# Add and GELU of two 1024 x 4096 matrices: which rows of HBM go to which partition

## The chip, the cores and the metric

The kernel runs on one core of a Trainium2 chip. The metric is the device time of one execution in microseconds. Three runs of the kernel before gave a median of 120.16 us (120.15 to 120.21).

## The reference

```python
batch, dim = 1024, 4096          # x, y: float32
z = x + y
return (0.5 * z * (1 + np.tanh(np.sqrt(2 / np.pi) * (z + 0.044715 * z ** 3)))).astype(np.float32)
```

Everything is elementwise: no value depends on its neighbours. Each of x, y and the output has 16.78 MB; 33.55 MB are read and 16.78 MB written.

## The kernel before, in words

Each matrix is seen as 128 rows of 128 KB, one row per partition: partition p holds the bytes from p x 128 KB on (`"(p n) d -> p (n d)"`). A row has TOT = 32768 floats, and HALF = 16384 floats is 64 KB. The tile z in SBUF has room for all of x and is overwritten by the sum and then by the result; the tile y holds half of y and is used twice.

There are six transfers, all issued from SyncE (SP), each 128 partitions of 64 KB, 8 MB in all. Their order is the list `sp`: first half of y (`load_y`, line 135), both halves of x (`load_x`, line 130), second half of y (line 135), first half of the output and second half (`store`, line 139). The second load of y waits until all adds that read the first half of y are done, because it writes the same tile. A store waits for the last GELU of its half. `begin_early` puts the issue of the first two loads ahead of the kernel's body; `wait_late` moves the wait for the last store behind the other end work.

The compute is cut into 20 chunks of 512 to 2048 columns. An add (line 150) is done by VectorE, or by GpSimd for chunks 7, 8 and 12. For eight chunks ScalarE copies x into PSUM first (`copy`, line 143), and the add reads that operand from PSUM. ScalarE then applies the GELU in place (line 162). The order on each engine is written out by hand in the lists `sp`, `pool`, `dve` and `acts`, and is issued under a manual schedule.

Of the kernel before, what the change touches and what calls it, by code (L numbers as in the profile page):

```python
# [66 lines left out]
def kernel(  # L67
# [12 lines left out]
    nc = tc.nc  # L80
    P = nc.NUM_PARTITIONS
# [3 lines left out]
    N, D = x.shape  # L85
    assert N % P == 0
    TOT = N // P * D
    xv, yv, ov = (a.rearrange("(p n) d -> p (n d)", p=P) for a in (x, y, out))

    HALF = TOT // 2  # L90
    xloads = [HALF, HALF]
    yloads = [16384, 16384]
    stores = [16384, 16384]
# [17 lines left out]
    def over(rs, lo, hi):  # L111
        return [i for i, (a, b) in enumerate(rs) if a < hi and b > lo]
# [6 lines left out]
    zt = pool_sb.tile([P, TOT], fp32, tag="z", name="z")  # L119
    yt = pool_y.tile([P, HALF], fp32, tag="y", name="y")  # L120
    ps = pool_ps.tile([P, 4096], fp32, tag="ps", name="ps")
# [5 lines left out]

    def load_x(i):
        a, b = xr[i]
        nc.sync.dma_start(out=zt[:, a:b], in_=xv[:, a:b])  # L130

    def load_y(i):
        a, b = yr[i]
        o = a % HALF
        nc.sync.dma_start(out=yt[:, o : o + b - a], in_=yv[:, a:b])  # L135

    def store(i):
        a, b = sr[i]
        nc.sync.dma_start(out=ov[:, a:b], in_=zt[:, a:b])

    def copy(c):
        a, b = cr[c]
# [2 lines left out]
    def add(c):  # L145
        a, b = cr[c]
        o = a % HALF
        eng = nc.gpsimd if c in on_gpsimd else nc.vector
# [15 lines left out]
    def earlier_user(c):  # L164
        lo, hi = copies[c], copies[c] + chunks[c]
        before = [k for k in copies if k < c and copies[k] < hi and copies[k] + chunks[k] > lo]
        return [(add, k) for k in before]

    sp = [(load_y, i) for i in over(yr, 0, HALF)] + [(load_x, 0), (load_x, 1)]
    sp += [(load_y, i) for i in over(yr, HALF, TOT)]  # L170
    sp += [(store, i) for i in range(len(stores))]
    pool = [(add, c) for c in on_gpsimd]
    dve = [(add, c) for c in on_vector]
# [3 lines left out]
        load_x: lambda i: [],  # L177
        load_y: lambda i: [(add, c) for c in over(cr, yr[i][0] - HALF, yr[i][1] - HALF)],
        copy: lambda c: [(load_x, i) for i in over(xr, *cr[c])] + earlier_user(c),
        add: lambda c: [(load_x, i) for i in over(xr, *cr[c])]  # L180
        + [(load_y, i) for i in over(yr, *cr[c])]
        + [(copy, k) for k in copies if k == c]
        + [(add, k) for h, k in held.items() if h == c],
# [55 lines left out]
```

## Time and profile before

| | us |
|---|---|
| median of three runs (lowest, highest) | 120.16 (120.15, 120.21) |
| span of the profiled execution, first to last instruction | 118.7 |
| median less span | 1.5 |
| VectorE busy | 29.1 |
| ScalarE busy | 44.1 |
| GpSimd busy | 13.8 |
| the DMA queue's packets, share of 16 DMA engines' span | 98.5% |
| issue to landing, median: y, x, output | 23.6, 50.1, 21.6 |
| HBM traffic over the span | 424 GB/s |

The profile is of one execution, and gives its span; of what lies around the span (1.5 us) it shows nothing, and the profiled execution has no time of its own beside the span. Busy time of an engine is time in which it executed; issues of DMAs are rows of SP's queue (SPq) and not busy time. "Landing" is when the semaphore of a transfer is complete. A window is a stretch of the span, with the busy time of each engine in it, the share of time in which the 16 DMA engines had a packet, and the GB/s.

### The profile page before, as it was taken

How to read it: one execution, taken by the hardware profiler on the slowest of the kernel's cores; microseconds unless marked ns; L12 is line 12 of the kernel's file. 1: busy time of each engine (PE TensorE's matmuls, PEld its weight loads, DVE VectorE, ACT ScalarE, POOL GpSimd, SP SyncE). 2: the span in 40 equal slices, each digit the busy share in tenths (PEclk: the TensorE clock that was granted, in tenths of full speed). 3: DMA queues.
4: the chain of work that ended last, by engine and by line, in shares of the span. 5: the costliest groups of instructions: out<-in, count | busy, mean ns of one | idle time of the engine just before them, and what ended most of it. 6: DMA issues, size and time to landing. Idle time of an engine off the chain costs nothing.

```text
span 118.7 us, 112 instructions
## 1 busy us (share of the span) xinstructions
DVE 29.1 (25%) x18; ACT 44.1 (37%) x30; POOL 13.8 (12%) x7
## 2 busy tenths in 40 slices
DVE  0000000000000099994000000009999920000000
ACT  5000000000000096792059999903799980000000
POOL 0000000000000029980000000009500000000000
DMA  9889988998899888998899888998899888988891
GB/s 353 353 375 641 398 353 353 596 464 353 353 420 618 376 353 353 618 442 353 353 508 552 353 353 375 641 398 353 353 552 508 353 353 353 707 353 353 353 641 66
DMA packets 864, 50.33 MB, mean 424 GB/s; under 512 B 96, under 2 KB 96, under 8 KB 96
## 3 DMA queue, kind: packets, MB, share of 16 engines
q1 hardware_dynamic: 864, 50.33, 98.5%
HBM read 33.55 MB, written 16.78 MB: 424 GB/s over the span
## 4 chain that ended last, share of the span: by engine, by line
DMA 56%; DVE 14%; ACT 10%; DVEq 1%; ACTq 0%; SPq 0%; issue 0%
DMA z<-in_x_dram 34%; DMA y<-in_y_dram 21%; DVE z L150 14%; ACT z L162 10%; DVEq L206 1%; ACTq L206 0%; SPq L135 0%; DVEq L150 0%
## 5 line engine op out<-in xcount | busy, mean ns | idle before, releaser
L162 ACT ACTIVATE z<-z 128x2048 f32<-128x2048 f32 (+3 forms) x20 | 29.7, 1555 | 5.5 <-DVE z L150 5.5
L143 ACT COPY ps<-z 128x2048 f32<-128x2048 f32 (+2 forms) x8 | 13.0, 1654 | 46.8 <-DMA z<-in_x_dram 45.1
L150 DVE TENSOR_TENSOR z<-z,y 128x2048 f32<-128x2048 f32 (+2 forms) x9 | 13.6, 1574 | 40.0 <-DMA z<-in_x_dram 40.0
L150 DVE TENSOR_TENSOR z<-ps,y 128x2048 f32<-128x2048 f32 (+2 forms) x8 | 15.6, 2016 | 25.4 <-DMA y<-in_y_dram 25.4
L150 POOL TENSOR_TENSOR z<-z,y 128x2048 f32<-128x2048 f32 x3 | 13.5, 4529 | 70.7 <-DVE z L150 43.4
L191 ACT ACT_TABLE_LOAD x1 | 1.3, 1283 | 1.3 <-PEq L223 1.3
L190 DVE MEMSET one<- 128x1 f32 x1 | 0.1, 59 | 1.3 <-PEq L223 1.3
L191 ACT ACTIVATE one<-one 128x1 f32<-128x1 f32 x1 | 0.2, 203 | 0.0
L223 POOL MEMSET const-float32-0.0<- 128x1 f32 x1 | 0.1, 99 | 0.2 <-issue 0.2
L223 POOL MEMSET const-bfloat16-1.0<- 128x1 bf16 x1 | 0.1, 102 | 0.0
L223 POOL MEMSET const-uint8-127<- 128x1 uint8 x1 | 0.1, 102 | 0.0
L223 POOL MEMSET const-float32-1.0<- 128x1 f32 x1 | 0.1, 99 | 0.0
## 6 DMA issues: line engine op xcount, KB each, us to landing
y<-in_y_dram SPq DMA_DIRECT2D x2, 23.6
z<-in_x_dram SPq DMA_DIRECT2D x2, 50.1
out_dram<-z SPq DMA_DIRECT2D x2, 21.6
```

The costliest lines, as they stand in the source:

```text
L143: nc.scalar.copy(out=in_psum(c), in_=zt[:, a:b])
L150: ins = eng.tensor_add(out=zt[:, a:b], in0=first, in1=yt[:, o : o + b - a])
L162: nc.scalar.activation(out=zt[:, a:b], in_=zt[:, a:b], func=act.Gelu_apprx_tanh)
L190: nc.vector.memset(one[:, :1], 0.0)
L191: nc.scalar.activation(out=one[:, :1], in_=one[:, :1], func=act.Gelu_apprx_tanh)
L206: tc.compile()
L223: nc = _bacc.Bacc("TRN2", target_bir_lowering=False, num_devices=1)
```

## The change

Half h of the columns of the tile now comes from another place in HBM. Partition p = 8q + j, with q from 0 to 15 and j from 0 to 7. Before, half h of partition p was the 64 KB at p x 128 KB + h x 64 KB. After, it is the 64 KB at q x 1 MB + h x 512 KB + j x 64 KB. So the eight partitions of a group still share 1 MB of each matrix, but half 0 of these eight partitions is the first 512 KB of it, without a gap, and half 1 the second 512 KB. x, y and the output are laid out alike. Nothing else is edited.

```diff
-    xv, yv, ov = (a.rearrange("(p n) d -> p (n d)", p=P) for a in (x, y, out))
-
     HALF = TOT // 2
+    Q = 16
+
+    def rows(array, lo, hi):
+        h = lo // HALF
+        assert hi <= (h + 1) * HALF
+        own = array.rearrange("n d -> (n d)").rearrange("(q h j c) -> h q j c", q=Q, h=2, j=P // Q)
+        return own[h][:, :, lo - h * HALF : hi - h * HALF]
+
...
     def load_x(i):
         a, b = xr[i]
-        nc.sync.dma_start(out=zt[:, a:b], in_=xv[:, a:b])
+        nc.sync.dma_start(out=zt[:, a:b], in_=rows(x, a, b))

     def load_y(i):
         a, b = yr[i]
         o = a % HALF
-        nc.sync.dma_start(out=yt[:, o : o + b - a], in_=yv[:, a:b])
+        nc.sync.dma_start(out=yt[:, o : o + b - a], in_=rows(y, a, b))

     def store(i):
         a, b = sr[i]
-        nc.sync.dma_start(out=ov[:, a:b], in_=zt[:, a:b])
+        nc.sync.dma_start(out=rows(out, a, b), in_=zt[:, a:b])
```

In the built program the pattern of a transfer was 128x16384 (rows by floats) on both sides. It is now 16x8x16384 on the HBM side, with 1 MB between the sixteen and 64 KB between the eight, and 128x1x16384 on the SBUF side.

## The prediction

> **What bounds the kernel now.** I read the page first: busy shares and slices, then the chain that ended last, then the windows cut at the landings, then the queue's own issues.
>
> ```profile
> span 118.7 us, 112 instructions
> DVE 29.1 (25%) x18; ACT 44.1 (37%) x30; POOL 13.8 (12%) x7
> DMA packets 864, 50.33 MB, mean 424 GB/s; under 512 B 96, under 2 KB 96, under 8 KB 96
> q1 hardware_dynamic: 864, 50.33, 98.5%
> ```
>
> No engine is busy for half the span, while the one queue's packets fill 98.5% of the time of 16 DMA engines. Take off the 96 tiny packets: 768 packets carry 50.33 MB, 65,536 bytes each. That is one packet for each 64 KB partition row of the six transfers (6 x 128), 48 on each DMA engine if they are dealt evenly. One takes about 0.985 x 16 x 118.7 / 768 = 2.44 us, which is 27 GB/s on one DMA engine.
>
> ```profile
> 4.20:21.90 17.70, 0.00 (x0) 0.00 (x0) 0.00 (x0) 1.00 1.08 467
> 21.90:41.30 19.40, 0.00 (x0) 0.00 (x0) 0.00 (x0) 1.00 1.00 432
> 41.30:60.70 19.40, 13.35 (x7) 11.21 (x7) 9.02 (x2) 1.00 1.00 432
> 60.70:80.10 19.40, 0.00 (x0) 16.39 (x10) 0.00 (x0) 1.00 1.00 432
> 80.10:99.40 19.30, 15.70 (x10) 15.01 (x11) 4.53 (x1) 1.00 1.00 435
> ```
>
> The last two columns are the DMA share and GB/s. (A packet is booked whole in the window where it starts, hence shares over 1.) One 8 MB transfer takes one window. It is 432 GB/s for loads, with or without VectorE, ScalarE and GpSimd at work beside it, and 435 for the store of the fifth window. A limit that is equal in both directions and blind to the engines lies in the path that loads and stores share, not in the direction of the HBM traffic, and it has no spare: share 1.00.
>
> ```profile
> 0.00 0.38 SPq L135 DMA_DIRECT2D y<-in_y_dram  x1
> 0.43 1.16 SPq L130 DMA_DIRECT2D z<-in_x_dram  x2
> 54.86 0.33 SPq L135 DMA_DIRECT2D y<-in_y_dram  x1
> 77.16 20.82 SPq L139 DMA_DIRECT2D out_dram<-z  x2
> ```
>
> The issues run ahead of the data. The second y load is issued at 54.86, while the second x load lands at 60.7; the first store goes out at 77.16, before the second y lands at 80.0; the second at 97.64, before the first store is through at 99.4. So the queue never runs dry. The kernel is a head of about 1 us, six transfers back to back, and a short tail: four loads at 19.4 and two stores at 19.3 make 116.2 of the 118.7 us, and 2.5 us are head and tail. The median of the runs is 120.16, 1.5 us over the span; that 1.5 is carried over unchanged. What the measurement can tell from no change is 0.2%, 0.24 us.
>
> **The change, part by part.** *Compute*: nothing. The listing of both programs has the same instructions on TensorE, VectorE, ScalarE and GpSimd in the same order with the same shapes; the function is elementwise, so it doesn't matter which row lies in which partition. Bytes, packet size (each run in a partition is still 64 KB), number of DMAs, their order and their waits are also the same. Cost 0, and there is no new wait.
>
> *The issue*: the pattern gets a dimension more (16x8x16384 on the HBM side, 128x1x16384 on the SBUF side, where both were 128x16384). What that costs SP no row shows. It could be nothing, or at most a second issue like the rows of 0.33 to 0.38 us; below nothing only if the queue had less to work out, and it has no less. I take 0.2 us, in the middle. Only the first issue is on the path, as the data can't start before it; the other five lie behind at least 1.8 us of queued data (97.64 against 99.4). So +0.2 us.
>
> *The deal of the rows to the DMA engines*: this is where the time is decided. Before, both sides of a transfer had an outer count of 128, one entry per partition. After, the HBM side has an outer count of 16, each entry a contiguous 512 KB, the size of exactly one DMA engine's share (128 rows over 16). If the queue cuts at the outermost count, engine q gets partitions 8q to 8q+7. The trace doesn't name an engine's partitions, so how it was before is not shown. What it shows is that the deal of before is as good as a deal can be: sixteen streams at 27 GB/s each, share 1.00, alike in both directions. This is what one gets if each of sixteen streams has an inlet into SBUF to itself. A deal that sends two streams through one inlet at a time gives each half of it, and leaves as many inlets idle. A packet then takes 4.84 us instead of 2.42, and a transfer 38.8 (stores 38.6). In a hardware path of equal shares the two stay in step for good: both come to the next inlet together.
>
> [...]
>
> The terms: the six transfers doubled, 4 x 38.8 + 2 x 38.6 = 232.4; head and tail 2.5; the issue 0.2; span 235.1. With the 1.5 us beside the span, 236.6, and I say 236.5. Is the compute still covered? The second y load waits for the first half's adds, 13.5 us after x lands (41.32 to 54.86). At half rate x lands at 80, so it is issued at 93.7, and the second x load fills the queue until 119: a cover of 25 us in place of 5.9. The first store goes out 16.4 us after the second x load (60.7 to 77.16), at 135, and y lands at 158. The second store goes out 17.6 us after that landing (80.0 to 97.64), at 175.6, with the first store moving until 197. So all compute is hidden deeper than before, and nothing of it adds to the sum.
>
> **The rivals.**
>
> *The pairs drift apart.* The halving needs partners that are always on the same inlet. If the eight rows of an engine spread over two inlets, and one partner is favoured or starts earlier, it moves ahead until it is on one inlet while the other is on the other. From four rows apart (4 x 2.42 = 9.7 us) nothing collides any more, and as the queue never runs dry the distance is not lost between transfers. Fully drifted at once: 120.2 + 9.7 + 0.2 = 130. Slowly: anything up to 228. For it: the streams do not start together (in the window from 1.00 to 4.20 only 369 GB/s are booked). Against it: a start apart by a fraction of a packet moves the pair by that fraction of four rows only, and the slowest pair ends the kernel. 0.15.
>
> *HBM collides instead.* Sixteen streams now start 1 MB apart, each walking 64 KB steps. Packets that get in each other's way are on record in the first window:
>
> ```profile
> 1.00:4.20 3.20, 0.06 (x1) 1.49 (x2) 0.00 (x0) 1.00 1.07 369
> ```
>
> 369 GB/s x 3.2 us are 18 packets, and 1.07 x 3.2 x 16 / 18 = 3.04 us for each, against 2.42 later. If every packet ran like these, 48 x 0.62 = 30 us come on top: 150. For: a big power of two between streams. Against: the step between rows was 128 KB before, a power of two as well, and nothing was lost after the first packets. 0.05 without the shared inlets. [...]
>
> *The deal doesn't matter.* If the queue deals as before, or the limit sits in each DMA engine and not at SBUF, six transfers take 116.2 us as now, and only the issue is left: 120.2 to 120.6. For it: 2.42 us a packet could as well be the engine's own pace. 0.12, half of it within 0.2%.
>
> *Faster, the other side.* Each DMA engine now reads one run of 512 KB. If that takes away what slows the first packets (3.04 against 2.42), the stream starts 0.6 us ahead, less 0.2 for the issue: 119.8. It decides as soon as it saves more than 0.2 + 0.24 us. Against anything larger: the packets after the first already run at share 1.00, so 2.5 us of head and tail are all there is. 0.08.
>
> **How the numbers follow.** Forecast 0.60 (228 to 241: an issue term of 0.38 and a first packet that doubles too make the upper end, a small drift the lower), drift 0.15, HBM 0.05, no matter 0.12, faster 0.08. The predicted time is the likeliest, 236.5. To hold 8 in 10 the range takes in forecast, drift and HBM: 130 to 241, and leaves out 0.20 at the fast end. The forecast's own range is 228 to 241. Faster 0.08, same 0.06, slower 0.60 + 0.15 + 0.05 + 0.06 = 0.86.
>
> **What would show it.** Right: still 768 large packets, DMA share near 1.00, windows of one transfer 38.8 us long at about 216 GB/s in both directions, x landing at about 80, compute rows unchanged in length. Drift: the first transfer at half rate and later ones faster. HBM: a loss that differs between loads and stores. No matter: landings at 41.3, 60.7 and 80.0 again. The forecast is wrong if a steady window still shows over 400 GB/s.

## The result, and the profile after

The changed kernel takes 237.98 us (median of 5 runs, 237.54 to 238.31) against 120.18 before: a ratio of 1.979, with a 95% interval of 1.976 to 1.983. The forecast was 236.5, with a range of 130 to 241; the forecast's own part of it was 228 to 241. The profiled execution took 237.54 us with a span of 236.0, so 1.5 us lie beside the span as before.

From the page of the changed kernel:

```profile
span 236.0 us, 112 instructions
DVE 29.1 (12%) x18; ACT 44.1 (19%) x30; POOL 13.8 (6%) x7
DMA packets 864, 50.33 MB, mean 213 GB/s; under 512 B 96, under 2 KB 96, under 8 KB 96
q1 hardware_dynamic: 864, 50.33, 98.6%
```

The same packets, the same bytes and the same compute to a tenth of a microsecond. The queue is as full as before (98.6%, before 98.5%), so the queue does not wait for work: each packet is open twice as long (0.986 x 16 x 236.0 / 768 = 4.85 us, before 2.44).

The windows of the changed kernel from the landing of its first load on, one for each further transfer (last two columns: DMA share, GB/s). The last edge between them, 197.80, lies 0.5 us before the first store lands:

```profile
43.40:83.90 40.50, 0.00 (x0) 0.02 (x1) 0.00 (x0) 1.00 1.00 207
83.90:124.30 40.40, 13.35 (x7) 11.19 (x7) 9.01 (x2) 1.00 1.00 208
124.30:164.60 40.30, 0.00 (x0) 16.39 (x10) 0.00 (x0) 1.00 0.95 208
164.60:197.80 33.20, 15.70 (x10) 15.01 (x11) 4.53 (x1) 1.00 1.04 247
197.80:236.00 38.20, 0.00 (x0) 0.00 (x0) 0.00 (x0) 1.00 0.88 197
```

These answer to the windows at 432 and 435 GB/s. A load takes 40.4 us where it took 19.4, with engines busy or idle. At 208 GB/s sixteen packets of 65,536 bytes pass in 5.04 us, against 2.43 at 432. The stores show a first one that is quicker and a second near half rate.

SP's issues in the changed kernel:

```profile
0.00 0.66 SPq L141 DMA_DIRECT2D y<-in_y_dram  x1
0.70 1.77 SPq L136 DMA_DIRECT2D z<-in_x_dram  x2
97.39 0.54 SPq L141 DMA_DIRECT2D y<-in_y_dram  x1
140.79 41.98 SPq L145 DMA_DIRECT2D out_dram<-z  x2
```

The first issue takes 0.66 us in place of 0.38. The second y load goes out at 97.4, with the queue full until 124.3, and the first store at 140.8, with y landing at 164.6: the compute is covered deeper than before (26.9 us in place of 5.9 for the second y load), as the sum had it with 25.

### The profile page after: what moved, and what is told of

Read it like the earlier page. It is cut to its first block, busy times and chain, and to the rows that moved or that the text cites. A ratio compares the mean times of both kernels' runs of the same rounds, so it can differ in the third digit from the quotient of the medians.

```text
span 236.0 us, 112 instructions
## 1 busy us (share of the span) xinstructions
DVE 29.1 (12%) x18; ACT 44.1 (19%) x30; POOL 13.8 (6%) x7
## 3 DMA queue, kind: packets, MB, share of 16 engines
q1 hardware_dynamic: 864, 50.33, 98.6%
HBM read 33.55 MB, written 16.78 MB: 213 GB/s over the span
## 4 chain that ended last, share of the span: by engine, by line
another core or an unknown queue 63%; DVE 7%; ACT 5%; DVEq 1%; ACTq 0%; issue 0%
DVE z L156 7%; ACT z L168 5%; DVEq L212 1%; ACTq L212 0%; DVEq L156 0%; DVE one L196 0%
```

## Experiments

The theory is that of the prediction (A): the outer count of 16 makes the queue give DMA engine q the partitions 8q to 8q+7, and then two engines stand at one SBUF inlet at a time. In the theory an inlet is a way into SBUF that several partitions share; partners are two engines whose partitions lie behind the same inlets; the deal is which partitions go to which engine. These are the author's assumptions: the runs set the outer count and show rates and DMA shares, and no trace shows an inlet or the partitions of an engine. Its rivals: (B) the HBM addresses, (C) the three-dimensional pattern as such, (D) an engine is slow on partitions that are not its usual ones, even alone.

**Groups of 4.**

```diff
-    Q = 16
+    Q = 32
```

> The changed kernel with 32 groups of 4 partitions in place of 16 groups of 8: the HBM runs stay contiguous (256 KB in place of 512 KB) and the pattern stays three-dimensional, but the outer count of 32 lets the queue deal groups of four. Theories: A, shared inlets (two DMA engines meet at one SBUF inlet, in step): every engine has its own inlet again, transfers of 19.4 us, time 120.16 plus the longer first issue (0.66 against 0.38 us in the profiles), 120.3 to 120.7. B, HBM addresses (contiguous runs, a big power of two between the engines): still slow, 150 to 238. C, the three-dimensional pattern makes each packet slow: 238. D, an engine that writes partitions other than its usual ones is slow even alone: as A.

Measured: 120.53 us, ratio to before 1.0041 (1.0026 to 1.0056). The windows of this kernel:

```profile
21.90:41.30 19.40, 0.00 (x0) 0.00 (x0) 0.00 (x0) 1.00 1.01 436
41.30:60.70 19.40, 13.35 (x7) 11.21 (x7) 9.03 (x2) 1.00 1.00 432
80.10:99.40 19.30, 15.70 (x10) 15.01 (x11) 4.53 (x1) 1.00 1.00 435
```

One number in the change carries the whole loss. HBM runs are still contiguous and the pattern still has three dimensions, so C falls, and B all but falls.

**Whole rows, 16 groups, and whole rows, 32 groups.** The layout goes, the outer count of 16 stays (by the theory the deal); then, with `Q = 32` besides, that goes too.

```diff
-        own = ....rearrange("(q h j c) -> h q j c", q=Q, h=2, j=P // Q)
+        own = ....rearrange("(j q h c) -> h q j c", q=Q, h=2, j=P // Q)
```

> The deal of the changed kernel (16 groups of 8 partitions) without its layout: partition 8q + j holds the whole 128 KB row 16j + q, so that no two partitions of a group are neighbours in HBM and the sixteen DMA engines read rows 128 KB apart. A, shared inlets: 236 to 239 us, transfers of 39 to 40 us. B, HBM addresses: 120 to 125 us, as the runs and the 1 MB steps are gone. C, pattern form: 238. D, far partitions: 238.

> The whole-row layout again (no neighbours in HBM within a group), with 32 groups of 4 partitions in place of 16 of 8. With the two kernels with contiguous runs and the whole-row kernel with 16 groups it closes a square of two layouts and two deals. A, shared inlets: 120.3 to 120.8 us, as the contiguous kernel with 32 groups (120.53). B, if contiguous runs are worth anything on their own: slower than that by more than 0.3 us.

Measured: 238.89 us with Q = 16 (one run), and 120.52 us with Q = 32 (ratio 1.0029, 1.0016 to 1.0043). A load window of each, first 16 groups, then 32:

```profile
84.00:124.00 40.00, 13.27 (x7) 11.06 (x7) 9.03 (x2) 1.00 1.01 210
```

```profile
41.30:60.70 19.40, 13.35 (x7) 11.21 (x7) 9.02 (x2) 1.00 1.01 439
```

The square of two layouts and two outer counts is closed: 16 groups cost 238 to 239 whatever the rows, 32 groups 120.5 whatever the rows. B is out, and the contiguous runs, the layout itself, are worth nothing that this measurement can tell.

**Loads only, stores only.** The other direction keeps the patterns of before. The edit of the loads-only kernel is shown; the other one does the same to the four loads.

```diff
-        nc.sync.dma_start(out=rows(out, a, b), in_=zt[:, a:b])
+        nc.sync.dma_start(out=ov[:, a:b], in_=zt[:, a:b])
```

> The four loads as in the changed kernel, the two stores as in the kernel before (so the output's rows go to other places than in the reference; everything is computed and stored). A, shared inlets: loads 40.4 us each as in the changed profile, stores 19.3: 4 x 40.4 + 2 x 19.3 + 2.9 + 1.5 = 204.6 us. B, if only HBM reads collide: the same; if only HBM writes: 121. C: 204.6.

> The four loads as in the kernel before, the two stores as in the changed kernel (the output's rows go to other places; everything is computed and stored). A, shared inlets: reads of SBUF share an inlet as writes do; by the changed profile's stores (33.9 and 39.3 us) 4 x 19.4 + 73.2 + 2.5 + 1.5 = 154.8 us, or 158.4 if the first store is as slow as the second. B, if HBM writes don't collide: 121. C: 155 to 158.

Measured: 204.56 us for the loads alone and 159.81 us for the stores alone, one run each. (With the expectation's own terms, two slow stores give 4 x 19.4 + 2 x 39.3 + 2.5 + 1.5 = 160.2 us, not 158.4.) Windows of the loads-only kernel, its last load and first store:

```profile
124.00:164.50 40.50, 0.00 (x0) 16.39 (x10) 0.00 (x0) 1.00 0.94 207
164.50:183.80 19.30, 15.70 (x10) 15.01 (x11) 4.53 (x1) 1.00 1.00 435
```

and of the stores-only kernel, its last load and both stores:

```profile
60.70:80.10 19.40, 0.14 (x1) 16.28 (x10) 0.13 (x1) 1.00 1.11 432
80.10:119.00 38.90, 15.56 (x10) 15.02 (x11) 4.41 (x1) 1.00 0.95 207
119.00:158.00 39.00, 0.00 (x0) 0.00 (x0) 0.00 (x0) 1.00 0.89 197
```

The loss follows the outer count of each transfer, switches from one transfer to the next, and is nearly the same for reading SBUF as for writing it (38.9 and 39.0 us for the two stores, 40.5 for a load). Here both stores are slow: the quick first store of the changed kernel is no property of stores.

**The issue alone.** The kernel before with its own patterns, and one switch of the program. The short form is here the issue as it stands in the profile before, 0.33 to 0.42 us each; the general form is the longer issue that the same transfers have with this edit:

```diff
     nc = tc.nc
+    nc.dge_precook = False
```

> The kernel before with one switch: its six transfers, with the same patterns of 128x16384, are issued in the general form and not in the short form that two-dimensional patterns get. It measures the issue term alone. If the 0.28 us by which the first issue is longer in the changed profile (0.66 against 0.38) is this form: first issue 0.6 to 0.7 us, time 120.4 to 120.6, transfers still 19.4. If the third dimension costs it: 120.16, first issue 0.38.

Measured: 120.51 us, ratio 1.0033 (1.0022 to 1.0045). Its first issues:

```profile
0.00 0.56 SPq L136 DMA_DIRECT2D y<-in_y_dram  x1
0.60 1.72 SPq L131 DMA_DIRECT2D z<-in_x_dram  x2
```

The longer issues, 0.56 and 0.47 us for the two y loads in place of 0.38 and 0.33, go with 0.40 us of the whole (0.0033 x 120.1; the interval gives 0.26 to 0.54). The first issue is 0.18 us longer here (0.56 against 0.38, where 0.6 to 0.7 was expected) and 0.28 us longer with the third dimension (0.66); where the rest lies was not settled. The two kernels with 32 groups, 1.0041 and 1.0029, and this one, 1.0033, have intervals that overlap, so a longer issue alone can account for the small loss of the 32-group kernels.

**Two engines, four engines.** If the outer count is the number of engines at work, two have 384 of the 768 packets each, and four have 192. That the two share no inlet, and that the four share theirs in pairs, was the author's assumption; no run shows it but by the rate.

```diff
-    Q = 16
+    Q = 2          # then 4
```

> [...] A, shared inlets: 2.42 us a packet, 384 packets each, 929 + 4 = 933 us. C, pattern form, and D, far partitions: 4.84 us and more a packet, 1860 us.

> [...] A, shared inlets: twice the engines of the two-engine kernel and no gain, 4.84 us a packet, 192 packets each, 929 + 4 = 933 us (up to 980 with the 5% by which the changed profile's packets are longer). If no inlet is shared: 2.42 us a packet, 469 us. C and D: 933.

Measured: 931.5 us with two and 744.2 us with four, one run each. The two-engine kernel in its middle third:

```profile
300.00:600.00 300.00, 13.35 (x7) 27.61 (x17) 9.03 (x2) 1.00 0.12 54
```

0.12 is 2/16: two engines at 27 GB/s each, at the pace that sixteen had before. Two engines moved all 128 partitions and neither was slowed by partitions that had been others' before: D is out. The four-engine kernel, every second stretch of 100 us:

```profile
2.00:100.00 98.00, 0.06 (x1) 1.49 (x2) 0.00 (x0) 1.00 0.25 56
200.00:300.00 100.00, 3.30 (x3) 3.38 (x2) 0.86 (x1) 1.00 0.25 62
400.00:500.00 100.00, 0.00 (x0) 16.39 (x10) 0.00 (x0) 1.00 0.25 68
600.00:700.00 100.00, 0.00 (x0) 0.00 (x0) 0.00 (x0) 1.00 0.25 92
```

Four engines (0.25 is 4/16) begin with what two of them moved, 56 against 54 GB/s, so 14 GB/s each in place of 27. By the theory, partners halve each other. But the rate climbs to 92, and the 933 us that were expected become 744. This fits partners that drift apart by themselves, the drift rival of the prediction, slowly; the trace shows the rate, not where each engine is.

**A head start for one of each pair.** Two more loads, ahead of all others, of 4 rows of 64 KB for each of 12 groups and then of 4 groups: 64 packets of 65,536 bytes, 4.19 MB, which the x loads overwrite. By the theory they put one engine of each pair 4 rows behind its partner. Which engines are partners, on which the edit and the expectation's 154.9 us rest, was the author's assumption:

```diff
+    def lead(k, first, lo):
+        own = x.rearrange(...)      # as in rows()
+        nc.sync.dma_start(out=zt[first : first + 4 * k, lo : lo + HALF], in_=own[0][:k, :4, :])
...
+    sp = [(lead, (12, 32, 0)), (lead, (4, 68, HALF))]
...
-    begin_early(nc, 2)
+    begin_early(nc, 3)
```

> [...] A, shared inlets with equal shares: partners are on different inlets for most of the time; a sum over sixteen engines that halves the pace of two on one inlet gives 154.9 us of transfers, so 157 to 170 us in all. If the partners slip back into step, or the halving has nothing to do with partners (B, C, D): 238 plus 10 to 20, 248 to 258.

Measured: 219.50 us, ratio 1.829 (1.825 to 1.833). It lies between the two expectations, so neither is right as it stands. Some of its windows:

```profile
45.00:70.00 25.00, 0.00 (x0) 0.00 (x0) 0.00 (x0) 1.00 1.00 336
70.00:95.00 25.00, 2.81 (x3) 2.86 (x2) 0.37 (x1) 1.00 1.02 343
95.00:105.60 10.60, 10.54 (x5) 8.35 (x6) 8.66 (x2) 1.00 0.56 235
107.50:127.00 19.50, 0.00 (x0) 8.46 (x6) 0.00 (x0) 1.00 0.96 205
127.00:147.00 20.00, 0.00 (x0) 7.94 (x5) 0.00 (x0) 1.00 0.96 216
```

and SP's issue of the second y load in this run:

```profile
105.62 0.54 SPq L145 DMA_DIRECT2D y<-in_y_dram  x1
```

From 45 to 95 us the transfers run at 336 to 343 GB/s with the outer count of 16 that gives 208 in the changed kernel. Then the DMA share falls to 0.56, while the second y load is held by the adds until 105.62; by the theory the engines ahead have then finished the x loads. When it comes, the rate is 205 GB/s again, as it would be with partners that start together. From 147 us on, where the stores begin, the windows stand at 341, 251 and 262 GB/s, so part of the loss goes once more. The last 19 us have a DMA share of only 0.48, which fits engines that no longer end together.

**The same without a wait that can empty the queue.** The adds and copies are left out, with and without the head start:

```diff
-    pool = [(add, c) for c in on_gpsimd]
-    dve = [(add, c) for c in on_vector]
+    pool = []
+    dve = []
...
-        gelu: lambda c: [(add, c)],
+        gelu: lambda c: [(load_x, i) for i in over(xr, *cr[c])],
```

> A control for the next kernel: the changed kernel without the adds and the copies into PSUM, so that the output is the GELU of x alone; y is loaded twice and not used. All six transfers keep their form and order, but the second y load waits only for the first, and each store only for the GELUs of its half, so the queue can't run dry. Every theory: transfers as in the changed kernel, 234 to 240 us.

> The kernel without adds plus the two extra loads that put one partner of each pair of DMA engines four rows behind. In the head-start kernel with the adds the queue ran dry for the engines ahead at 105.6 us, where the second y load was waiting for adds, and the partners started again together. Here no transfer waits for adds. A, shared inlets: the distance is kept to the end; 154.9 us of transfers by the halving sum, 4 to 8% more for the overhead seen while sharing: 158 to 175 us, with 300 GB/s and more in every window after the first 45 us. If partners slip back into step by themselves: 230 to 258 us.

Measured: 237.82 us without the head start, and 177.51 us with it, one run each. A window without it:

```profile
95.00:120.00 25.00, 0.00 (x0) 3.38 (x2) 0.00 (x0) 1.00 1.01 210
```

From the page and the windows of the kernel with it:

```profile
DMA packets 944, 54.53 MB, mean 310 GB/s; under 512 B 112, under 2 KB 112, under 8 KB 112
2.00:45.00 43.00, 0.06 (x1) 1.49 (x2) 0.00 (x0) 1.00 0.96 197
45.00:70.00 25.00, 0.00 (x0) 0.00 (x0) 0.00 (x0) 1.00 1.02 343
70.00:95.00 25.00, 0.00 (x0) 3.69 (x3) 0.00 (x0) 1.00 1.01 346
95.00:120.00 25.00, 0.00 (x0) 15.10 (x11) 0.00 (x0) 1.00 1.03 354
120.00:145.00 25.00, 0.00 (x0) 10.60 (x8) 0.00 (x0) 1.00 0.97 401
```

It moves 4.19 MB more in 60 us less. From 45 to 145 us no second collapse comes: the same transfers run at 343 to 401 GB/s after the two extra loads and at 210 without them. So the half rate is fixed neither by the pattern nor by the rows nor by the engines, and depends on what ran before; the theory, by which it matters who stands at which inlet when, fits this. The time is 2.5 us over the expected 158 to 175. Two things cost time: the head start is itself bought at 197 GB/s for the first 43 us, and up to 120 us the rate is 343 to 354 and not 432; by the theory, partners still meet for part of the time. How much of the miss belongs to which was not worked out.

## Why the prediction was right, point by point

- *What bounds it* held: the queue's share is 98.6% and no compute came to the surface.
- *The deal* held as far as rates can show it, by the square of layouts and outer counts, the single directions, and the head start; only the first 5 us of the first store do not follow it (last section). No run shows an inlet, its equal halves or the partitions of an engine, on which the sum's 4.84 us a packet rests; what the runs showed in its place is 208 GB/s, or 5.04 us a packet, with 16 groups, and 432 to 436 GB/s with 32. Nor does a run show which partners meet. On it rest the 933 us expected of two and of four engines, which took 931.5 and 744.2 us, and the 154.9 us in the expectations of both head-start kernels, which took 219.50 and 177.51 us. That the outer count sets how many engines work fits the DMA shares of 0.12 and 0.25 for outer counts of 2 and 4.
- *The price* was mis-sized twice, in opposite directions. A load took 40.4 us, not 38.8: the pace was less than half, 5.04 us a packet in place of 4.84, and four loads make +6.4 us. The stores took 71.3 us together (164.7 to 236.0), not 77.2: -5.9, because the first one ran fast at its start. The close hit is in part luck, as these two cancel: with two stores of 38.6 us the time would have been 237.98 + 5.9 = 243.9 us, above the 241 at which the range ended.
- *The issue*: 0.40 us measured (0.26 to 0.54), 0.2 taken; 0.38 was the upper bound, by the row of one whole issue, and that was about the size. The profiles show 0.18 to 0.28 of it in the first issue.
- *Drift* had 0.15 and did not come within this kernel's loads: 207, 208, 208 GB/s. The rise of the four-engine kernel's rate from 56 to 92 GB/s fits it. In the first store there is little of it once its quick start is over:

```profile
167.60:197.80 30.20, 12.80 (x8) 13.87 (x10) 1.65 (x1) 1.00 1.06 237
```

  A packet takes 1.06 x 16 x 65,536 bytes / 237 GB/s = 4.7 us there, against 5.04 in the loads and 2.43 before. The sentence that the distance is not lost because the queue never runs dry did not hold in the head-start kernel: its DMA share fell to 0.56 before the waits of the kernel released the second y load at 105.62 us, and the rate was 205 GB/s after it.
- *HBM* and *faster* are out: the same addresses, or nearly, at 432 to 436 GB/s with 32 groups, and no gain for contiguous runs. *The deal doesn't matter* is out by the result.

## What to carry to other kernels

The outer count of a DMA's pattern can decide the rate of a transfer: here an outer count of 16 (237.98 us) in place of 128 (120.18) or 32 (120.53) doubled the time with every byte, every packet and all compute the same. That it does so by the way the rows are dealt to the DMA engines is a theory that the rates fit and no trace shows. A transfer that runs at half rate with the DMA share still at 1.00, as these loads did at 208 GB/s, can be tested by changing the outermost count alone, before looking at HBM. The loss went and came back within one kernel (336 to 343 GB/s, and 205 after the wait for the adds), so read the rate by windows, not by its mean.

## What the runs showed of the hardware

- Two engines that share an inlet, by the theory, lose more than half: 208 GB/s for 16 engines, where half of 432 is 216.
- The first store starts at nearly full rate after loads with the new pattern (419 GB/s), whereas after loads with the old one its packets are slow at once (4.8 us). The first 5 us of the first store, in the changed kernel and then in the stores-only kernel:

```profile
162.60:167.60 5.00, 2.89 (x3) 1.14 (x2) 2.88 (x1) 1.00 1.00 419
```

```profile
79.10:84.10 5.00, 4.14 (x3) 2.12 (x2) 4.13 (x1) 1.00 1.50 328
```

A packet counts whole where it starts. In 5 us at a share of 1.00 the first has 2.1 MB, two packets for each engine; the share of 1.50 at 328 GB/s in the second stands for 1.6 MB in packets of 1.50 x 5.0 x 16 / 25 = 4.8 us. The kernel without adds, also with the new pattern in its loads, has 237 GB/s from 145 to 176 us, between 210 before and 210 after; by an estimate from these rates its 33.55 MB of loads end there, at about 164 us, and its first store begins. The theory says that partners meet from the first row on, so it does not explain this, and why the first store starts quicker was not settled.
- Why the rate climbs by itself with four engines (56 to 92 GB/s) and stays at 207 to 208 GB/s in sixteen engines' loads was not settled either.
